# Later chunks of x, copies plus accumulating transfers in the first out-projection, a moved decay array, and w_down's copies at another place in the queue

## The chip, the core and the metric

The kernel runs on one core of one Trainium2 chip. Its engines work side by side, each on its own list of instructions in order: TensorE (PE, matrix products; PEld are its weight loads), VectorE (DVE), ScalarE (ACT), GpSimd (POOL) and SyncE (SP, which here only issues transfers). The metric is the device time of one execution in microseconds (us), as the median of several runs.

## The reference

One decoder layer on x with 2048 positions and 1024 channels, all in float32:

```python
h = rms_norm(x, norm1_g)
z = einsum('bsd,de->bse', h, w_in)              # 1024 -> 3584
lru_x, lru_gate, sc_b, sc_c, sc_x = split(z)    # 1024, 1024, 512, 512, 512
lru_x = causal_dwconv(lru_x, lru_conv_w) + lru_conv_b
y_lru = rg_lru(lru_x, ...) * gelu(lru_gate)     # gated linear recurrence over positions
y_sc = sc_b * causal_dwconv(sc_c * sc_x, sc_conv_w)
x = x + einsum('bse,ed->bsd', concat(y_lru, y_sc), w_out)    # 1536 -> 1024
h = rms_norm(x, norm2_g)
u = causal_dwconv(einsum('bsd,df->bsf', h, w_up), ffn_conv_w)    # 1024 -> 6144
gate, up = split(u)
x = x + einsum('bsf,fd->bsd', gelu(gate) * up, w_down)      # 3072 -> 1024
return rms_norm(x, final_g)
```

## The kernel before

Positions are worked in two halves of 1024 (T), and these in blocks of 512 (NB); channels lie on the 128 partitions. Every product is made exact enough by splitting both operands into a high part, a rounded copy by ScalarE (L233, names wh, fh, xh), and a low part, the difference by VectorE (L234, names wl, fl, xl), and adding three matmuls: high by high, high by low, low by high. So TensorE waits for a weight until a transfer (wr, wrw, wrf), ScalarE and VectorE have all done their part.

The stages, with the stretch of the profile: w_in for half 0 (0 to 337 us, `in_phase`, 28 products of 48 matmuls), the first out-projection (337 to 456), w_in for half 1 (456 to 752, `in_blocks`), the second out-projection (752 to 870), then w_up and w_down for half 0 and for half 1 (888 to 2250), and a tail. The stages after the first use a scheme with seven products of 2x2 blocks in place of eight; it needs sums of weight blocks and of operand blocks. The sums of w_out and w_down (so_d, sd_d) are made in HBM: `sum_step` has SyncE copy a block to its place and, two copies later, GpSimd add another block to it by an accumulating transfer (L409, L412). Each product of w_in's first stage calls `sum_step` once; for w_down, each pair j of the up stage calls it twice.

**In `in_phase`**, `beside_first(n)` stands beside the n-th product. It also makes the mean square of half 1 of x, in eight chunks xs0 to xs7 of 128 channels: load the chunk into one of two pages of 128 x 1024 (L1076, pages taken in turn by n % 2), square it (ScalarE, L1070 and L1072), add it up (VectorE, L1073, into ss_a). After the last it splits the sum, multiplies it by ones (four matmuls, ms_a) and takes the inverse root (`inv_rms`, a ScalarE table function ry_a and four VectorE operations). The loads stand in SyncE's queue between loads of w_in's weights (wr_in, L249).

**An out-projection (`sweeps`)** has seven sweeps of three steps. A step loads a weight block and an operand block (L1017), splits both, and does 24 matmuls into four PSUM banks (L1004). Odd sweeps go on adding into the same four banks (ox); even ones use banks of their own (oy). At a sweep's end its banks are added to or taken from the result pages xr (L1041, VectorE), which were loaded with x beforehand (`x_residual`, L586, SyncE):

```python
TAKEN = [[("11", 1, False)], [("12", 1, False), ("22", -1, False)],
         [("12", 1, False)], ...
```

"11", "12", "21" and "22" name the four quarters of the result, in two pages each (xr_11_0, xr_11_1); the first sweep is added to 11, the second to 12 and taken from 22. The loads of xr for 11 stand in the first sweep, those for 22 and 12 in the second, those for 21 in the last. Beside the steps, operands of a later stage are made (`x1_beside`, names hax, hbx, hcx; in the second out-projection `h_beside`, names ha, hb, at steps 4, 10, 15 and 19). `lru_scan` of the last channel group of half 1 runs at the opening of the second out-projection: its decay array a lies in one of two pages with tag "b", which xr_12's two pages use too.

The order of each engine's list is set by priorities (`high_priority(offset=...)`): an instruction with a larger offset is put as if it had been written so much earlier. Pages with a tag and a number of buffers (bufs) make a load wait until the last reader of the page's old contents is done, and SyncE's queue, being in order, holds all that stands behind such a load.

Of the kernel before, what the change touches and what calls it, by code (L numbers as in the profile page):

```python
# [14 lines left out]
S = 2048  # L15
# [16 lines left out]
GP = 0  # L32
UPP = 200
CP = 160
NS = 2
J0 = 2
LEAD = 5
# [56 lines left out]
def block_kernel(  # L94
# [282 lines left out]
    def lru_scan(c, half, cv, g, *gates, home=None, sign=1.0):  # L377
        n = f"{half}_{c}"
        r, i = (flat(p(f"{x}{n}")) for p, x in zip(home or (act, act), "ri"))
        a = big(f"a{n}", c % 2)[:, :T] if home else flat(act(f"a{n}"))  # L380
        with tc.high_priority(offset=HP):
            for k, (rows, ps) in enumerate(zip(HALVES, gates)):
                for b, p in enumerate(ps):
                    for dst, o, at in ((r, O_BA, k), (i, O_BX, 1 - k)):
                        nc.scalar.activation(
                            dst[rows, blk(b)], p[HALVES[at], :], AF.Sigmoid, bias=col(o + c)[rows, :]
                        )
        nc.vector.tensor_tensor(i, i, cv, ALU.mult)
        m = cv
        nc.scalar.activation(a, r, AF.Exp, scale=nc8[:, c : c + 1])  # L390
        nc.scalar.activation(m, r, AF.Tanh, scale=c8[:, c : c + 1])
        nc.scalar.activation(r, a, AF.Square)
        nc.vector.scalar_tensor_tensor(m, r, 1.0, m, ALU.add, ALU.mult)
        nc.scalar.activation(m, m, AF.Sqrt)
        nc.vector.tensor_tensor(i, i, m, ALU.mult)
        h = r
        init = 0.0 if half == 0 else h_last[:, c : c + 1]
        nc.vector.tensor_tensor_scan(h, a, i, init, ALU.mult, ALU.add)
        if half < NH - 1:
            nc.vector.tensor_copy(h_last[:, c : c + 1], h[:, T - 1 : T])  # L400
        nc.scalar.activation(g, g, AF.Gelu_apprx_tanh, scale=sign)
        y = g if home else h
        nc.vector.tensor_tensor(y, g, h, ALU.mult)
        return y
# [172 lines left out]
    def res_page(name, side):  # L577
        return ub.tile([P, 2, NB], F32, name=name, tag="ab"[side], bufs=2)

    def x_residual(half, alloc):  # L580
        def get(key, p):
            mh, t = PLACE[key]
            r = alloc(key, f"xr{half}_{key}_{p}")
            c = 4 * mh + 2 * p
            o = half * T + t * NB
            nc.sync.dma_start(r, xT[c : c + 2, :, o : o + NB].rearrange("m p c -> p m c"))  # L586
            return r

        return get

    def store_pair(dst, t, r, when=1):
        defer(when, dst[:, :, blk(t)].rearrange("m p c -> p m c"), r)
# [189 lines left out]
            a, c = even.pop()  # L782
            combine_odd(f_d[half], when, j // 2, a, cu, c, (cg[:, :NB], cg[:, NB:]))

    def up_phase(half, hs, between):
        with tc.high_priority(offset=UPP):
            wts = [up_weights(half, 0)]
        wts.append(up_weights(half, 1))
# [1 line left out]
        for j in range(NFF):  # L790
            if j + 2 < NFF:
                wts.append(up_weights(half, j + 2))
            nxt = UpPair(half, j + 1, hs, wts[j + 1]) if j + 1 < NFF else None
            if j == 0:
                cur.spread()
                nxt.begin()
                nxt.sum1()
            elif nxt is None:
                cur.middle(cur.sum1)
                cur.second()  # L800
                cur.fourth()
                cur.end()
            else:
                cur.middle(cur.second)
                nxt.begin()
                cur.fourth()
                if j + 2 < NFF:
                    nxt.sum1()
                cur.end()
            up_rest(half, j, cur.ug, cur.un)  # L810
            cur = nxt
            between(j)
# [169 lines left out]
                add = src[W_OPS.index(b), i2] if b in W_OPS else flat(dst[b][i2])  # L982
                pieces.append((t, src[W_OPS.index(a), i2], add))

    def sweeps(half, wsrc, fsrc, ni, name, residual, done, beside, tail=0, lead=0):
        res = {}
        fetch = {}
        for key, at in (("11", ((0, 1), (0, 2))), ("22", ((1, 0), (1, 0))), ("12", ((1, 2), (1, 2))), ("21", ((6, 1), (6, 1)))):
# [3 lines left out]
        for s, (wo, fo, on_x) in enumerate(SWEEPS):  # L992
# [42 lines left out]
            for m in range(4):  # L1035
                for h in held:
                    mm((m,), *h)
                for key, sign, final in TAKEN[s]:
                    r = res[key][m // 2][:, m % 2, :]
                    with tc.high_priority(offset=HE if not last else 2 * HP if m == 3 else HP):  # L1040
                        nc.vector.tensor_tensor(r, r, ps[m], ALU.add if sign > 0 else ALU.subtract)  # L1041
                    if final:
# [21 lines left out]
    def beside_first(n):  # L1064
        if n == 0:
            ss1[1] = acc_tile("a1")
        if 1 <= n <= KC:
            t = x1_raw.pop(n - 1)
            if n == 1:
                nc.scalar.activation(ss1[1], t, AF.Square)  # L1070
            else:
                nc.scalar.activation(t, t, AF.Square)  # L1072
                nc.vector.tensor_tensor(ss1[1], ss1[1], t, ALU.add)  # L1073
        if n < KC:
            t = x1_raw[n] = big(f"xs{n}", n % 2)[:, :T]
            nc.sync.dma_start(t, xT[n, :, T:S])  # L1076
        if n == KC:
            x1_raw["mean"] = mean_split(ss1[1], "a1")
        if n == KC + 2:
            inv_rms(ss1[1], "a1", x1_raw["mean"])  # L1080
        if n == -1:
            hx.append(x1_prep(0, ss1[1], 1))
# [31 lines left out]
    def res_alloc(key, n):  # L1114
# [9 lines left out]
        x_residual(0, res_alloc),  # L1124
        store_done(x2_d[0], None, "b0"),
        x1_beside,
    )

    rs2 = [[], []]
# [51 lines left out]

        return beside

    prepare = h_beside(0, (4, 10, 15, 19))

    def out1_beside(s):
        if s == 0:
# [12 lines left out]
        store_done(x2_d[1], None, "b1"),  # L1200
        out1_beside,
        lead=LEAD,
    )

    sums(w_down, sd_d, NI)
    mean1 = squares_then_mean(lambda k: x2_d[1][k // 2][k % 2], "b1", rs2[1], 2)

    def beside_pairs(j):
        mean1(j)
        for _ in range(NS if j >= J0 else 0):  # L1210
            sum_step()

    up_phase(0, hs[0], beside_pairs)

    ss3 = acc_tile("c0")

# [151 lines left out]
```

## Time and profile before

| what | value |
|---|---|
| median of 3 runs (lowest, highest) | 2262.89 us (2262.66, 2264.75) |
| profiled execution | 2264.07 us, its span 2262.3 us |
| mean granted clock of TensorE | 0.996 |
| TensorE, VectorE, ScalarE, GpSimd busy | 98%, 79%, 54%, 8% of the span |
| DMA queues: SyncE's, GpSimd's share of 16 engines | 45.7%, 9.5% |

In the profile a row of a timeline begins with its start and length in us, then engine, line, operation, output and inputs by the program's names with buffer numbers left out, and the number of instructions merged into it. In brackets stands how long the engine was idle just before, and what it waited for; "issue" means that the profile shows no reason. SPq is SyncE's queue. Adjacent rows of an engine may overlap by some 0.1 us, since the end of an instruction overlaps the next one's start.

### The profile page before, as it was taken

Reading aid. Unit: us, or ns where it says so; the run is one execution under the profiler, and the core shown is the slowest. Engines: PE = TensorE matmul, PEld = TensorE weight load, DVE = VectorE, ACT = ScalarE, POOL = GpSimd, SP = SyncE. Lnnn points to the kernel's source line nnn. Section 1 sums busy time; section 2 is a strip of 40 time slices with the busy share of each in tenths; the row PEclk is TensorE's granted clock in tenths of the full one; section 3 lists DMA queues with packets and bytes.
Section 4 is the critical chain, followed back from the end, with each engine's and each line's share of the span. In section 5 each row is a group of like instructions: output and inputs, shape, how many; then the busy total and the mean of one; then the engine's idle time right before and its main releaser. Section 6 shows DMA issues by size and latency. Waiting matters only on the chain.

```text
span 2262.3 us, 26386 instructions
## 1 busy us (share of the span) xinstructions
PE 2227.1 (98%) x9754; PEld 1818.2 (80%) x9754; DVE 1787.4 (79%) x2070; ACT 1214.6 (54%) x1404; POOL 174.1 (8%) x298
## 2 busy tenths in 40 slices
PE   9999999999999899999999999999999999999997
PEld 7787787888777688888888888888888888888886
DVE  8867879947777899898888887677988888876556
ACT  7638834547798554555454444444544444453343
POOL 0011110000100100111211100000000000000000
PEclk9999999999999999999999999999999999999999
DMA  7476357833533875588773267674233232359764
GB/s 281 149 228 188 110 212 267 305 100 125 186 117 109 310 258 184 163 251 236 209 179 112 98 216 269 228 252 147 88 104 118 91 111 93 112 194 345 246 196 153
DMA packets 157952, 415.00 MB, mean 183 GB/s; under 512 B 16640, under 2 KB 19328, under 8 KB 157248
## 3 DMA queue, kind: packets, MB, share of 16 engines
q1 hardware_dynamic: 136960, 356.96, 45.7%
q0 software_dynamic: 20720, 56.37, 9.5%
q8 instruction: 76, 1.25, 0.2%
q14 instruction: 52, 0.43, 0.1%
q10 hardware_dynamic: 144, 0.00, 0.0%
HBM read 311.55 MB, written 139.46 MB: 199 GB/s over the span
## 4 chain that ended last, share of the span: by engine, by line
PE 82%; DVE 6%; issue 6%; ACT 4%; DMA 2%; POOL 0%; SPq 0%; DVEq 0%; ACTq 0%; POOLq 0%
PE zx L671 21%; PE dx L1004 12%; PE zc L671 10%; PE zin_b L289 10%; PE dy L1004 9%; PE za L671 5%; PE ox L1004 5%; PE oy L1004 3%; PE zxin L671 2%; PE zS L671 1%; PE zcin L671 1%; PE zW L671 1%; DMA wrc_up<-in_w_up 1%; PE zain L671 1%; PE zr_b L374 1%
## 5 line engine op out<-in xcount | busy, mean ns | idle before, releaser
L234 DVE TENSOR_TENSOR fl_d<-wrf_d,fh_d 128x1024 fp32r<-128x1024 f32 x84 | 102.8, 1224 | 122.3 <-ACT fh_d L233 120.0
L233 ACT ACTIVATE fh_d<-wrf_d 128x1024 fp32r<-128x1024 f32 x84 | 89.0, 1059 | 202.1 <-PE dy L1004 78.5
L1004 PE MATMUL dx<-fh_d,wl_d 128*128 128x512 f32 x384 | 149.4, 389 | 0.0
L1004 PE MATMUL dx<-fl_d,wh_d 128*128 128x512 f32 x384 | 149.4, 389 | 0.0
L1004 PE MATMUL dx<-fh_d,wh_d 128*128 128x512 f32 x384 | 149.4, 389 | 0.0
L289 PE MATMUL zin_b<-xh,wl_in 128*128 128x512 f32 x448 | 138.8, 391 | 2.6 <-DVE wl_in L234 2.6
L289 PE MATMUL zin_b<-xh,wh_in 128*128 128x512 f32 x448 | 140.1, 394 | 0.0
L289 PE MATMUL zin_b<-xl,wh_in 128*128 128x512 f32 x448 | 138.9, 391 | 0.0
L234 DVE TENSOR_TENSOR wla_up<-wra_up,wha_up 128x1024 fp32r<-128x1024 f32 x48 | 58.8, 1225 | 100.9 <-ACT wha_up L233 100.9
L350 DVE SCALAR_TENSOR_TENSOR cg<-ug,prm,cg 128x1024 f32<-128x1024 f32 x96 | 123.1, 1282 | 9.4 <-ACT cg L346 8.5
L350 DVE SCALAR_TENSOR_TENSOR cu<-un,prm,cu 128x1024 f32<-128x1024 f32 x96 | 122.8, 1280 | 4.7 <-ACT cu L346 4.3
L671 PE MATMUL zc<-hhB,whd_up 128*128 128x512 f32 x368 | 120.8, 389 | 0.0
L671 PE MATMUL zx<-ht,whc_up 128*128 128x512 f32 x368 | 113.3, 389 | 0.0
L1004 PE MATMUL dy<-fh_d,wl_d 128*128 128x512 f32 x288 | 112.0, 389 | 0.0
L1004 PE MATMUL dy<-fl_d,wh_d 128*128 128x512 f32 x288 | 112.0, 389 | 0.0
L1004 PE MATMUL dy<-fh_d,wh_d 128*128 128x512 f32 x288 | 112.0, 389 | 0.0
L682 ACT ACTIVATE ug<-zx 128x512 f32<-128x512 f32 x92 | 54.8, 596 | 102.5 <-PE zx L671 102.1
L234 DVE TENSOR_TENSOR wl_d<-wrw_d,wh_d 128x1024 fp32r<-128x1024 f32 x84 | 102.5, 1220 | 8.4 <-ACT wh_d L233 7.0
L289 PEld LDWEIGHTS zin_b<-xh,wh_in 128*128 128x128 f32 x448 | 84.0, 189 | 23.4 <-DVE xl L425 1.5
L289 PEld LDWEIGHTS zin_b<-xh,wl_in 128*128 128x128 f32 x448 | 84.6, 189 | 20.7 <-DVE wl_in L234 3.1
L289 PEld LDWEIGHTS zin_b<-xl,wh_in 128*128 128x128 f32 x448 | 84.5, 189 | 18.0 <-DVE xl L458 0.4
L233 ACT ACTIVATE wha_up<-wra_up 128x1024 fp32r<-128x1024 f32 x48 | 50.9, 1060 | 82.8 <-PE zx L671 76.0
(549 smaller groups left out, 6384.4 us busy)
## 6 DMA issues: line engine op xcount, KB each, us to landing
wrc_up<-in_w_up SPq DMA_DIRECT2D x48, 512.0 KB, 4.9
f_d_T<-cg SPq DMA_DIRECT2D x96, 256.0 KB, 2.6
wrw_d<-sd_d_S SPq DMA_DIRECT2D x48, 512.0 KB, 4.5
wrf_d<-f_d_T SPq DMA_DIRECT2D x48, 512.0 KB, 4.2
f_d_B<-cu SPq DMA_DIRECT2D x72, 256.0 KB, 2.5
wrw_d<-in_w_down SPq DMA_DIRECT2D x36, 512.0 KB, 4.9
wrf_d<-f_d_B SPq DMA_DIRECT2D x36, 512.0 KB, 3.5
wr_in<-in_w_in SPq DMA_DIRECT2D x25, 512.0 KB, 7.1
```

The lines of the kernel that those rows point to most:

```text
L233: nc.scalar.activation(r32(hi), src, AF.Copy)
L234: nc.vector.tensor_tensor(r32(lo), src, hi, ALU.subtract)
L289: nc.tensor.matmul(ps[t], r32(a), r32(b[:, blk(t)]), start=(first and i == 0), stop=(last and i == 2))
L350: nc.vector.scalar_tensor_tensor(dst, src[:, k : k + T], col(o_w + k), dst, ALU.mult, ALU.add)
L374: nc.tensor.matmul(ps[t], gw[rows, :], cv[rows, blk(t)], start=True, stop=True)
L671: nc.tensor.matmul(ps, r32(p[:, s]), r32(self.hs[k][x][o]), start=f and i == 0, stop=l and i == 2, skip_group_check=True,)
L682: nc.scalar.activation(dst, self.x, AF.Copy)
L1004: nc.tensor.matmul(ps[m], r32(p), r32(x[:, k, :]), start=first and i == 0 and n == 0, stop=(last or not on_x) and i == ni - 1 and n == 2, ...
```

## The change

Four edits:

1. The loads of xs are no longer made beside products 0 to 7 but 0, 1, 3, 4, 5, 6, 7, 8; the mean's split comes beside product 9 and the inverse root beside product 11 (8 and 10 before).
2. In the first out-projection, the results 11, 12 and 22 get no load of x. At their first sweep, ScalarE copies the banks into the pages, with the sign as scale, and GpSimd then adds x to each page by an accumulating transfer from HBM. Six loads of SyncE and twelve adds of VectorE become six such transfers and twelve copies. Result 21, and the whole second out-projection, stay as they were.
3. The decay array of the last channel group's scan in half 1 is put into a page of another pool (`vpage`), away from xr_12's pages; the first `h_beside` of the second out-projection comes at step 5, not 4.
4. The two `sum_step`s of w_down stand ahead of the mean's loads (`mean1`) in an up pair, rather than behind them and the pair's other work beside it, and begin one pair later (j = 3, not 2).

```diff
+LATE = (("11", "12", "22"), ())
+LASTA = NLRU - 1
+XS_AT = (0, 1, 3, 4, 5, 6, 7, 8)
+XS_SIDE = 0
+XS_INV = 11
...
     def lru_scan(c, half, cv, g, *gates, home=None, sign=1.0):
-        a = big(f"a{n}", c % 2)[:, :T] if home else flat(act(f"a{n}"))
+        a = big(f"a{n}", c % 2)[:, :T] if home and c < LASTA else flat((act if not home else vpage)(f"a{n}"))
...
     def x_residual(half, alloc):
         def get(key, p):
             r = alloc(key, f"xr{half}_{key}_{p}")
-            nc.sync.dma_start(r, xT[c : c + 2, :, o : o + NB].rearrange("m p c -> p m c"))
+            if key not in LATE[half]:
+                nc.sync.dma_start(r, x_block(half, key, p))
             return r
+    def x_fills(half):
+        def fill(key, p, r):
+            nc.gpsimd.dma_start(r, x_block(half, key, p), accum_op=ALU.add)
+        return fill
...
-    def up_phase(half, hs, between):
+    def up_phase(half, hs, between, behind=lambda j: None):
...
             if j + 2 < NFF:
                 wts.append(up_weights(half, j + 2))
+            behind(j)
...
                 for key, sign, final in TAKEN[s]:
                     r = res[key][m // 2][:, m % 2, :]
+                    if fills and key in LATE[half] and not any(k == key for k, _, _ in sum(TAKEN[:s], [])):
+                        with tc.high_priority(offset=HE):
+                            nc.scalar.activation(r, ps[m], AF.Copy, scale=float(sign))
+                        if m % 2 == 1:
+                            fills(key, m // 2, res[key][m // 2])
+                        continue
...
     def beside_first(n):
-        if 1 <= n <= KC:
-            t = x1_raw.pop(n - 1)
-            if n == 1:
+        if n - 1 in XS_AT:
+            k = XS_AT.index(n - 1)
+            t = x1_raw.pop(k)
+            if k == 0:
...
-        if n < KC:
-            t = x1_raw[n] = big(f"xs{n}", n % 2)[:, :T]
-            nc.sync.dma_start(t, xT[n, :, T:S])
-        if n == KC:
+        if n in XS_AT:
+            k = XS_AT.index(n)
+            t = x1_raw[k] = big(f"xs{k}", (n + XS_SIDE) % 2)[:, :T]
+            nc.sync.dma_start(t, xT[k, :, T:S])
+        if n == XS_AT[-1] + 1:
             x1_raw["mean"] = mean_split(ss1[1], "a1")
-        if n == KC + 2:
+        if n == XS_INV:
             inv_rms(ss1[1], "a1", x1_raw["mean"])
...
-    prepare = h_beside(0, (4, 10, 15, 19))
+    prepare = h_beside(0, (5, 10, 15, 19))
...
-    def beside_pairs(j):
-        mean1(j)
-        for _ in range(NS if j >= J0 else 0):
+    def down_sums(j):
+        for _ in range(NS if j > J0 else 0):
             sum_step()
-    up_phase(0, hs[0], beside_pairs)
+    up_phase(0, hs[0], mean1, down_sums)
```

The change moves instructions on several engines; three places show how. First SyncE's queue in `in_phase`, around the third load of xs. Before (wr_in_21, wr_in_25 and so on are weights of w_in's products, so_d the copies for w_out's sums):

```order
L249 DMA wr_in_21_985<-in_w_in 128x1024
L409 DMA so_d_S_2_221<-in_w_out 16x8192
L1076 DMA xs_1045<-in_xT 128x1024
L249 DMA wr_in_25_1052<-in_w_in 128x1024
L409 DMA so_d_S_0_216<-in_w_out 16x8192
L249 DMA wr_in_17_1124<-in_w_in 128x1024
L409 DMA so_d_S_1_217<-in_w_out 16x8192
L249 DMA wr_in_2_1200<-in_w_in 128x1024
```

The same place in the changed kernel:

```order
L254 DMA wr_in_21_985<-in_w_in 128x1024
L414 DMA so_d_S_2_221<-in_w_out 16x8192
L254 DMA wr_in_25_1050<-in_w_in 128x1024
L414 DMA so_d_S_0_216<-in_w_out 16x8192
L254 DMA wr_in_17_1122<-in_w_in 128x1024
L414 DMA so_d_S_1_217<-in_w_out 16x8192
L254 DMA wr_in_2_1198<-in_w_in 128x1024
L414 DMA so_d_S_2_218<-in_w_out 16x8192
L1100 DMA xs_1268<-in_xT 128x1024
```

The third load of xs has gone from ahead of three weight loads to behind them.

Second, VectorE's list at the end of the first out-projection's second sweep. Before (oy_1 are that sweep's banks; wl_o and fl_o the low parts of the weight and operand of the step whose sweep and number follow; hlB, hlT and htx split operands of half 1's products):

```order
L234 TENSOR_TENSOR hlT1x_2867<-hcx_2852,hhT1x_2866 128x1024
L234 TENSOR_TENSOR htx_2870<-hqx_2853,htx_2870 128x512
L1041 TENSOR_TENSOR xr_12_0_2926<-xr_12_0_2926,oy_1_0_2802 128x512
L1041 TENSOR_TENSOR xr_22_0_2818<-xr_22_0_2818,oy_1_0_2802 128x512
L1041 TENSOR_TENSOR xr_12_0_2926<-xr_12_0_2926,oy_1_1_2803 128x512
L234 TENSOR_TENSOR wl_o_2_0_2967<-wrw_o_2_0_2962,wh_o_2_0_2966 128x1024
L1041 TENSOR_TENSOR xr_12_1_2928<-xr_12_1_2928,oy_1_2_2804 128x512
L234 TENSOR_TENSOR fl_o_2_0_2971<-wrf_o_2_0_2964,fh_o_2_0_2970 128x1024
L1041 TENSOR_TENSOR xr_22_1_2820<-xr_22_1_2820,oy_1_2_2804 128x512
L234 TENSOR_TENSOR wl_o_2_1_3003<-wrw_o_2_1_2998,wh_o_2_1_3002 128x1024
```

The same place in the changed kernel:

```order
L239 TENSOR_TENSOR wl_o_2_0_2967<-wrw_o_2_0_2962,wh_o_2_0_2966 128x1024
L239 TENSOR_TENSOR hlB11x_2857<-hax_2844,hhB11x_2856 128x1024
L239 TENSOR_TENSOR hlB21x_2861<-hbx_2845,hhB21x_2860 128x1024
L239 TENSOR_TENSOR hlT1x_2865<-hcx_2850,hhT1x_2864 128x1024
L239 TENSOR_TENSOR fl_o_2_0_2971<-wrf_o_2_0_2964,fh_o_2_0_2970 128x1024
L239 TENSOR_TENSOR wl_o_2_1_3003<-wrw_o_2_1_2998,wh_o_2_1_3002 128x1024
L239 TENSOR_TENSOR htx_2868<-hqx_2851,htx_2868 128x512
```

The adds into xr are gone from ahead of fl_o_2_0, and wl_o_2_0 now stands before the operands for half 1.

Third, GpSimd's list behind the last stores of y (y_d) of half 0. In the changed kernel:

```order
L235 DMA y_d_T_2_98<-yc_10_2509 128x512
L602 DMA xr_11_0_2734<-in_xT 128x2x512
L602 DMA xr_11_1_2771<-in_xT 128x2x512
L602 DMA xr_12_0_2924<-in_xT 128x2x512
L602 DMA xr_22_0_2818<-in_xT 128x2x512
L602 DMA xr_12_1_2925<-in_xT 128x2x512
L602 DMA xr_22_1_2819<-in_xT 128x2x512
L235 DMA x_d_0_263<-xr_12_0_2924 128x2x512
```

The six L602 rows are new here; before, the first x_d store followed the y_d store.

More of the change, by code (lines that the diff above doesn't have):

```diff
@@ L578, in res_page, with x_block @@
         return ub.tile([P, 2, NB], F32, name=name, tag="ab"[side], bufs=2)
+    def x_block(half, key, p):
+        mh, t = PLACE[key]
+        c = 4 * mh + 2 * p
+        o = half * T + t * NB
+        return xT[c : c + 2, :, o : o + NB].rearrange("m p c -> p m c")
     def x_residual(half, alloc):
         def get(key, p):
-            mh, t = PLACE[key]
             r = alloc(key, f"xr{half}_{key}_{p}")
-            c = 4 * mh + 2 * p
-            o = half * T + t * NB
-            nc.sync.dma_start(r, xT[c : c + 2, :, o : o + NB].rearrange("m p c -> p m c"))
-            return r
-        return get
+            if key not in LATE[half]:
+                nc.sync.dma_start(r, x_block(half, key, p))
+            return r
+        return get
+    def x_fills(half):
+        def fill(key, p, r):
+            nc.gpsimd.dma_start(r, x_block(half, key, p), accum_op=ALU.add)
+        return fill
     def store_pair(dst, t, r, when=1):
@@ L983, in sums, with sweeps @@
                 pieces.append((t, src[W_OPS.index(a), i2], add))
-    def sweeps(half, wsrc, fsrc, ni, name, residual, done, beside, tail=0, lead=0):
+    def sweeps(half, wsrc, fsrc, ni, name, residual, done, beside, tail=0, lead=0, fills=None):
         res = {}
@@ L1126, in block_kernel @@
         x1_beside,
+        fills=x_fills(0),
     )
@@ L1202, in block_kernel @@
         lead=LEAD,
+        fills=x_fills(1),
     )
```

## The prediction

> **What bounds the kernel now.** I read the busy shares on the page first, then the list of TensorE's waits, then the timelines around the longest of them.
>
> ```profile
> PE 2227.1 (98%) x9754; PEld 1818.2 (80%) x9754; DVE 1787.4 (79%) x2070; ACT 1214.6 (54%) x1404; POOL 174.1 (8%) x298
> PE oy L1004 <- DVE fl_o L234: 4.7, 3, 2.5
> PE ox L1004 <- DVE fl_o L234: 3.6, 2, 2.6
> PE zin_b L289 <- DVE wl_in L234: 2.6, 1, 2.6
> ```
>
> The first row gives busy time and share of each engine; the others give what TensorE waited for, in us altogether, times, and the longest. TensorE is busy for 2227.1 of 2262.3 us and no matmul is added or taken away, so the change can only win back waits and what they cause. The three rows hold 10.9 us: six waits, one while w_in's halves are multiplied, five in the two out-projections. Each is for VectorE to make the low part of an operand (wl_in or fl_o), so VectorE's order there decides, and whatever holds up VectorE.
>
> **Part 1: the chunks of x.** The queue's wait, and VectorE, ScalarE and TensorE around it:
>
> ```profile
> 46.70 0.69 DVE L277 TENSOR_TENSOR sb<-wr,sb 128x512 f32<-128x512 f32 x1
> SPq L1076 <- ACT ss_a L1070: 59.0, 1, 59.0
> 91.72 0.34 SPq L1076 DMA_DIRECT2D xs<-in_xT  x1
> 92.16 0.38 SPq L249 DMA_DIRECT2D wr_in<-in_w_in  x1
> 90.65 1.04 ACT L1070 ACTIVATE ss_a<-xs 128x1024 f32<-128x1024 f32 x1
> 102.13 1.06 ACT L233 ACTIVATE wh_in<-wr_in 128x1024 fp32r<-128x1024 f32 x1 [4.08 <-DMA wr_in<-in_w_in]
> 103.39 1.22 DVE L234 TENSOR_TENSOR wl_in<-wr_in,wh_in 128x1024 fp32r<-128x1024 f32 x1
> 104.66 0.73 PE L289 MATMUL zin_b<-xh,wl_in 128*128 128x512 f32 x2 [2.63 <-DVE wl_in L234]
> ```
>
> SyncE's queue issues nothing for 59.0 us: its third xs load needs the buffer of the first, which ScalarE's square frees only at 90.65 + 1.04 = 91.69. The weights queued behind it leave at 92.16 and land at about 102.1, which sets the split and TensorE's 2.63 us wait. In the new order this xs load stands behind three weight loads; the raw pages that the first two of these take are last read by the column sums around 46.70, so they go some 44 us earlier, and the third has two products, over 20 us, to spare. The wait goes, and the slower restart after it (0.1 us: 0.50 for the first matmul after a wait in the rows of part 2, where 0.39 is usual): 2.7.
>
> The wait has a second price:
>
> ```profile
> 103.00:110.00 7.00, 5.34 (x16) 4.26 (x17) 7.00 (x11) 3.37 (x4) 2.02 (x3) 0.76 1.03 383
> 160.00:252.00 92.00, 92.00 (x402) 71.81 (x402) 74.51 (x87) 78.25 (x82) 15.13 (x26) 1.00 0.55 160
> ```
>
> These are windows: length, busy time of each engine with its instructions, TensorE's granted clock, DMA share, GB/s. At full clock a matmul takes 92/402 = 0.229 us. After the wait 16 matmuls fill 110 - 104.66 = 5.34 us in place of 3.66: 1.7 us lost to a granted clock of 0.76 over the window. **Part 1 is worth 2.7 + 1.7 = 4.4 us.** The Trainium skill, page "TensorE: Matmul & The Clock Gate", section "Part 1: The HAM clock gate", says that the clock halves after at least one idle window of about 3.4 us, on a free-running grid. By it a wait of 2.63 us leaves the clock alone and this part gives only 2.7; the row shows the clock dropped, so the row decides.
>
> The shift also drags x's mean and inverse root (four DVE operations, 2 x 0.6 and 2 x 1.2 = 3.6 us, and a ScalarE table load) to the opening of the first out-projection, ahead of and around the third step's fl_o. Replayed with the durations of the rows, that fl_o ends about 0.2 us before TensorE asks for it. I take 0.3 us of wait, bounds 0 and 1.3 (one more operation ahead of it).
>
> **Part 2: the first out-projection's evictions.** In the profile:
>
> ```profile
> 351.34 2.05 DVE L1041 TENSOR_TENSOR xr<-xr,ox 128x512 f32<-128x512 f32 x3 [1.26 <-PE ox L1004]
> 358.63 1.22 DVE L234 TENSOR_TENSOR fl_o<-wrf_o,fh_o 128x1024 fp32r<-128x1024 f32 x1
> 359.91 0.50 PE L1004 MATMUL oy<-fl_o,wh_o 128*128 128x512 f32 x1 [0.90 <-DVE fl_o L234]
> 368.86 1.88 DVE L1041 TENSOR_TENSOR xr<-xr,oy 128x512 f32<-128x512 f32 x3 [1.51 <-PE oy L1004]
> 372.39 1.22 DVE L234 TENSOR_TENSOR fl_o<-wrf_o,fh_o 128x1024 fp32r<-128x1024 f32 x1
> 373.66 0.50 PE L1004 MATMUL ox<-fl_o,wh_o 128*128 128x512 f32 x1 [2.58 <-DVE fl_o L234]
> ```
>
> VectorE runs in order. Ahead of 351.34 and of 368.86 it stands idle 1.26 and 1.51 us until a product is finished, then adds it to x, and only then splits the operand that TensorE needs next. TensorE waits 0.90 and 2.58 us, and each restart costs a further 0.1: 3.7 together. In the new order the twelve adds are gone from VectorE, and with them 12 x 0.6 = 7.2 us. The second sweep's first fl_o (372.39 now) then waits only for ScalarE's half; replayed it ends near 367.7, while TensorE reaches it at 373.66 - 3.7 = 370.0. **Worth 3.7 us.** Below: 0, if ScalarE's copies make the fh_o late instead; against it stands
>
> ```profile
> L682 ACT ACTIVATE ug<-zx 128x512 f32<-128x512 f32 x92 | 54.8, 596 | 102.5 <-PE zx L671 102.1
> 350.00:400.00 50.00, 46.52 (x204) 37.90 (x203) 46.85 (x54) 22.93 (x24) 0.00 (x0) 1.00 0.69 233
> ```
>
> a copy of this shape at 596 ns, 12 x 0.6 = 7.2 us on an engine with 22.93 busy of 50, where VectorE has 46.85.
>
> What it adds: six transfers from GpSimd's queue that add x to the copies in place (512 KB each), for six plain loads that go. The trace has none into on-chip memory. The nearest are the accumulating transfers that add up weights in HBM, of the same size:
>
> ```profile
> 85.29 0.94 POOL L412 DMA_DIRECT2D so_d_S<-in_w_out  x1
> 92.00 0.90 POOL L412 DMA_DIRECT2D so_d_S<-in_w_out  x1 [5.77 <-issue]
> 103.94 0.88 POOL L412 DMA_DIRECT2D so_d_S<-in_w_out  x1 [11.04 <-issue]
> 956.12 0.95 POOL L412 DMA_DIRECT2D sd_d_S<-in_w_down  x1 [0.50 <-issue]
> 962.27 0.92 POOL L412 DMA_DIRECT2D sd_d_S<-in_w_down  x1 [5.20 <-DVE whd_up L234]
> so_d_S<-in_w_out POOLq DMA_DIRECT2D x5, 512.0 KB, 10.0
> sd_d_S<-in_w_down POOLq DMA_DIRECT2D x12, 512.0 KB, 6.1
> ```
>
> The last two rows are counts, size and median us to landing. One such transfer does not start before the last has landed: they start 6.7 and 11.9 us apart in the first stage, 6.15 in the second. So with L us from issue to landing, n of them take n x L + 0.3(n - 1). The three that matter are 12_0, 22_0 and 12_1, in this order, which can start when ScalarE has copied the second sweep's first products, about 369.5 on the clock of the rows above. VectorE adds the third sweep's products to page 12_1 in order, at about 387.3 (the sweep's 72 matmuls end near 386.1, and two adds of 0.6 stand before it). Behind those adds stands the fl_o for the second step of the fourth sweep: TensorE reaches it 24 matmuls, 5.4 us, after 386.1, at 391.5, and without a wait it ends at 386.1 + 4 x 0.6 + 1.2 = 389.7. There are 1.8 us to spare, so 12_1 must land by 389.1: 369.5 + 3L + 0.6 = 389.1, L = 6.3. Above that TensorE waits 3(L - 6.3).
>
> L depends on the load:
>
> ```profile
> 85.00:133.00 48.00, 45.37 (x194) 37.04 (x193) 42.56 (x52) 14.82 (x14) 8.20 (x12) 0.96 0.95 294
> 956.00:1062.00 106.00, 106.00 (x469) 87.78 (x468) 95.80 (x108) 56.77 (x68) 17.65 (x35) 1.00 0.83 231
> 368.00:391.00 23.00, 20.42 (x90) 16.61 (x89) 21.77 (x26) 8.28 (x9) 0.00 (x0) 1.00 0.70 240
> q0 software_dynamic: 3808, 7.34, 34.5%
> ```
>
> With 0.95 of the DMA engines busy the median is 10.0, with 0.83 it is 6.1. The last row is the accumulating queue's share over 950 to 1085, in which 14 were issued: 0.345 x 135/14 = 3.3 us of all 16 engines each. From 368 to 391 the share is 0.70 without them; three add 10 us to 16.1, which is all that 23 us can hold, though a part of the weight loads can slip. I take L = 7.3, between the two and nearer to the second, so 3 us of wait, bounds L = 5.6 (no wait) and 11.6 (16 us). The Trainium skill, page "DMA: Bandwidth & Descriptors", section "Anatomy of one DMA — SWDGE (gpsimd) path", fits 2.0 us plus the bytes over 436 GB/s to such a queue's transfers: an estimate of 3.2 us here and no wait. No transfer of this size and kind in this trace landed near that.
>
> **Part 3: the second out-projection.**
>
> ```profile
> 767.45 5.11 SPq L586 DMA_DIRECT2D xr<-in_xT  x2
> 772.61 0.46 SPq L1017 DMA_DIRECT2D wrw_o<-so_d_S  x1
> 776.76 0.50 PE L1004 MATMUL oy<-fl_o,wh_o 128*128 128x512 f32 x1 [2.51 <-DVE fl_o L234]
> 782.55 1.23 DVE L234 TENSOR_TENSOR fl_o<-wrf_o,fh_o 128x1024 fp32r<-128x1024 f32 x1
> 783.83 0.50 PE L1004 MATMUL oy<-fl_o,wh_o 128*128 128x512 f32 x1 [1.29 <-DVE fl_o L234]
> 790.55 0.50 PE L1004 MATMUL ox<-fl_o,wh_o 128*128 128x512 f32 x1 [0.99 <-DVE fl_o L234]
> ```
>
> The second x load of the pair stood until the scan let go of the page that its decay array held; with the array elsewhere the weights behind it leave about 4 us earlier. In the new order the fl_o of 782.55 stands ahead of the four adds of xr_11 (2.4 us at 0.6 each), and h's first chunk comes a step later: the 783.83 wait goes, 1.4 with its restart. The 776.76 wait hangs on the scan, which still runs before it; the 790.55 one on stores of y. Both stay. **Worth 1.4**, bounds -1.3 (the chunk moves its delay on to the next step) and 2.7.
>
> **Part 4: w_down's copies**, moved by a pair and ahead of the sx loads, stand between the same stores and the same w_up loads. TensorE's wait there is
>
> ```profile
> 1113.08 0.50 PE L671 MATMUL zx<-hhB,whc_up 128*128 128x512 f32 x1 [1.50 <-ACT ug L682]
> ```
>
> I take 0: the copies go out behind a pair's matmuls, and without that cover cost about another such wait. Bounds -1.6 and +1.6.
>
> **Sum.** -4.4 + 0.3 - 3.7 + 3 - 1.4 = -6.2 on the profiled run's 2264.07 (span 2262.3 and 1.8 around it): 2257.9. That run lies 1.2 above the median 2262.89, so I predict **2256.7**. One halved-clock window more or less is 1.7.
>
> **Rivals.** *No wait for the fills* (L up to 6.3, as between 956 and 1062): 2256.7 - 3 - 0.3 = 2253.4. For it: six plain loads leave the stretch or the one before it. Against: the 10 us of DMA time.
> *Fills at the crowded rate*, L 8.5 to 9.5: waits of 6.6 to 9.6, with a halved window 8.3 to 11.3 against the 3 above: 2262 to 2265, no change. For it: the 10.0 row.
> *Slower: fills one by one in a full queue.* The mechanism is the same in-order add of 12_1 ahead of fl_o; without any fill wait the sum is 2253.7, so it loses once the wait and its clock pass 9.2 us, L near 8.8, and is clearly slower (2267.4) from L near 10.3. At the 11.6 of the rows 92.00 to 103.94: 16 + 1.7 more, 2271.4. Against it: that stretch held 0.95 before one fill came, this one 0.70.
> *The change doesn't cure the out-projection*: VectorE, at 46.85 of 50, is late by its operand chain, not by the adds, or the copies hold up fh_o: the 3.7 stays and the sum is 2260.4, no change. Against it: its idle 1.26 and 1.51 just before the adds.
>
> **Chances.** Forecast 0.42, no wait 0.22, crowded 0.15, slower 0.11, not cured 0.10. A measurement tells 0.2%, 4.5 us: faster is below 2258.4. The forecast's own range, 2254 to 2260, lies below it for most of its chance (0.35 of 0.42), all of the second does, and 0.03 of the others: 0.60. Slower 0.12, the rest 0.28. The range 2250.5 to 2264.5 holds the forecast, the second and the two that end level, and leaves out the slower one and the tails.
>
> **What would show it.** Right: no wait for wl_in near 104 and a clock of 1.00 in that window; SyncE issuing weights between 48 and 90; no fl_o wait in the first two sweeps' steps near 359 and 373; GpSimd rows of xr<-in_xT six to eight us apart; a wait for fl_o near 390 of about 3 us. Wrong: GpSimd's fills far apart (slow) or issued back to back (no chain at all); a new wait in the opening steps at 345 to 350; clock drops elsewhere, as at the 776.76 wait, which now costs none.

## The result: slower by 0.4%, and the profile after

| | before | changed |
|---|---|---|
| median of 4 runs each, us | 2263.82 (2262.66 to 2265.41) | 2274.24 (2272.87 to 2275.10) |
| profiled execution and its span, us | 2264.07, 2262.3 | 2273.72, 2271.9 |
| ratio of the runs, 95% interval | | 1.0037 (1.0022 to 1.0051) |

The changed kernel is slower by 8.4 us by the ratio (5.0 to 11.5; the medians of the table differ by 10.4). 2256.7 was forecast, in a range of 2250.5 to 2264.5, and the time lies above it. Measured from the first matmul of each stage to that of the next in the two traces, the difference of the spans, 9.6 us, goes where this table puts it:

| stage | before | changed | difference |
|---|---|---|---|
| w_in, half 0 | 331.1 | 326.3 | -4.8 |
| first out-projection | 118.3 | 129.2 | +10.9 |
| w_in, half 1 | 296.9 | 296.3 | -0.6 |
| second out-projection | 120.0 | 120.3 | +0.3 |
| w_up, half 0 | 459.8 | 464.2 | +4.4 |
| everything after | 930.4 | 929.9 | -0.5 |

The page and the list of TensorE's waits of the changed kernel:

```profile
PE 2229.6 (98%) x9754; PEld 1819.2 (80%) x9754; DVE 1778.9 (78%) x2058; ACT 1219.0 (54%) x1415; POOL 183.6 (8%) x304
PE oy L1020 <- DVE fl_o L239: 13.9, 3, 11.1
PE zx L686 <- ACT ug L697: 3.9, 2, 2.5
PE ox L1020 <- DVE fl_o L239: 1.4, 3, 0.8
```

The wait for wl_in is gone from the list, the waits for ox fell from 3.6 to 1.4 us, and one wait for oy of 11.1 us is new. Three views show what that one is: GpSimd's timeline, then VectorE's and TensorE's, then four windows.

```profile
348.33 1.25 POOL L602 DMA_DIRECT2D xr<-in_xT  x1 [22.98 <-ACT xr L1058]
358.91 1.23 POOL L602 DMA_DIRECT2D xr<-in_xT  x1 [9.33 <-ACT hhT1x L238]
370.51 1.19 POOL L602 DMA_DIRECT2D xr<-in_xT  x1 [10.38 <-PE ox L1020]
380.78 1.20 POOL L602 DMA_DIRECT2D xr<-in_xT  x1 [9.08 <-ACT wh_o L238]
390.62 1.19 POOL L602 DMA_DIRECT2D xr<-in_xT  x1 [8.64 <-ACT wh_o L238]
396.99 1.20 POOL L602 DMA_DIRECT2D xr<-in_xT  x1 [5.17 <-issue]
383.07 1.27 DVE L1063 TENSOR_TENSOR xr<-xr,ox 128x512 f32<-128x512 f32 x2
396.76 1.28 DVE L1063 TENSOR_TENSOR xr<-xr,ox 128x512 f32<-128x512 f32 x2 [12.42 <-DMA xr<-in_xT]
397.96 1.22 DVE L239 TENSOR_TENSOR fl_o<-wrf_o,fh_o 128x1024 fp32r<-128x1024 f32 x1
387.72 0.39 PE L1020 MATMUL oy<-fh_o,wh_o 128*128 128x512 f32 x1
399.24 0.79 PE L1020 MATMUL oy<-fl_o,wh_o 128*128 128x512 f32 x1 [11.13 <-DVE fl_o L239]
```

The six rows of xr<-in_xT are the accumulating transfers 11_0, 11_1, 12_0, 22_0, 12_1 and 22_1. Each is issued some 0.3 us after the one before it has landed: 10.6, 11.6, 10.3, 9.8 and 6.4 us apart. VectorE has added to page 12_0 at 383.07 and then stands for 12.42 us at the add to 12_1, whose transfer was issued only at 390.62 and landed at 396.67. The fl_o behind that add ends at 399.2, and TensorE, which had nothing left to do from 388.1 (387.72 + 0.39), goes on in the same instant. The columns of the windows are length, busy time of PE, PEld, DVE, ACT and POOL with instructions, granted clock, DMA share, GB/s:

```profile
340.00:360.00 20.00, 20.00 (x90) 16.51 (x89) 19.73 (x20) 11.74 (x14) 2.34 (x2) 1.00 0.75 229
370.00:381.00 11.00, 10.36 (x45) 7.93 (x44) 10.21 (x11) 9.30 (x11) 1.41 (x2) 1.00 1.02 337
391.00:397.00 6.00, 0.00 (x0) 0.00 (x0) 0.24 (x1) 0.00 (x0) 0.83 (x2) 0.50 0.67 122
398.00:404.00 6.00, 4.76 (x11) 3.80 (x12) 6.00 (x7) 0.00 (x0) 0.19 (x1) 0.50 0.80 180
```

Up to 360 TensorE never stops. While the DMA engines are full (1.02) a transfer takes 9.5 to 11.3 us from issue to landing; when SyncE's queue has nearly run dry (0.67, of which its own transfers are 0.08) the fifth takes 6.05. The granted clock also halves during the wait, and TensorE pays for that until 404: 11 matmuls in the last row, 4.76 us after it restarted, where full speed gives 21.

### The profile page after: what moved, and what is told of

Read it like the earlier page. It is cut to its first block, busy times and chain, and to the rows that moved or that the text cites. A ratio compares the mean times of both kernels' runs of the same rounds, so it can differ in the third digit from the quotient of the medians.

```text
span 2271.9 us, 26392 instructions
## 1 busy us (share of the span) xinstructions
PE 2229.6 (98%) x9754; PEld 1819.2 (80%) x9754; DVE 1778.9 (78%) x2058; ACT 1219.0 (54%) x1415; POOL 183.6 (8%) x304
## 3 DMA queue, kind: packets, MB, share of 16 engines
q0 software_dynamic: 22352, 59.52, 10.3%
## 4 chain that ended last, share of the span: by engine, by line
PE 77%; issue 7%; DVE 6%; ACT 6%; DMA 3%; POOL 1%; SPq 1%; DVEq 0%; POOLq 0%; ACTq 0%
PE zx L686 20%; PE dx L1020 11%; PE zc L686 10%; PE dy L1020 9%; PE zin_b L294 8%; PE za L686 5%; PE ox L1020 3%; PE oy L1020 3%; PE zxin L686 3%; DMA wrc_up<-in_w_up 1%; PE zcin L686 1%; PE zS L686 1%; ACT r L390 1%; PE zW L686 1%; PE zain L686 1%
## 5 line engine op out<-in xcount | busy, mean ns | idle before, releaser
L238 ACT ACTIVATE fh_d<-wrf_d 128x1024 fp32r<-128x1024 f32 x84 | 89.0, 1059 | 205.5 <-PE dy L1020 78.5
L355 DVE SCALAR_TENSOR_TENSOR cg<-ug,prm,cg 128x1024 f32<-128x1024 f32 x96 | 122.8, 1279 | 10.6 <-ACT cg L351 9.8
```

The source lines that it names most:

```text
L238: nc.scalar.activation(r32(hi), src, AF.Copy)
L355: nc.vector.scalar_tensor_tensor(dst, src[:, k : k + T], col(o_w + k), dst, ALU.mult, ALU.add)
```

## The experiments

Each kernel was timed in turns with the kernel before on the same chip; ratios are to that kernel, with 95% intervals, and 0.1% is 2.3 us. A diff is against the changed kernel, unless it is said to be added to the kernel before; `...` stands for lines left out.

### One edit at a time

The first edit alone, as what has to be taken back from the changed kernel:

```diff
-LATE = (("11", "12", "22"), ())
+LATE = ((), ())
-LASTA = NLRU - 1
+LASTA = NLRU
-    prepare = h_beside(0, (5, 10, 15, 19))
+    prepare = h_beside(0, (4, 10, 15, 19))
...
-    up_phase(0, hs[0], mean1, down_sums)
+    up_phase(0, hs[0], beside_pairs)
```

> The kernel before with the first edit alone (chunks of x at products 0, 1, 3 to 8, mean and inverse root a product later). Theory, from the two profiles: the first stage shortens from 331.1 to 326.3 us and nothing else moves, so 4 to 5 us faster than before, about 0.998. Rival: the mean and inverse root that now run at the opening of the first out-projection push its operand splits back, and part or all of the gain is lost there: 0 to 3 us faster.

Measured: 0.9979 (0.9971 to 0.9988), 4.8 us faster. Its first stage takes 326.3 us, as in the changed kernel, and at the opening of the first out-projection, where the mean's work now stands, TensorE does not stop (first row). The wait of 0.90 us at the second sweep's first fl_o, which part 2 of the prediction counts, is gone with this edit too. What is left is the wait of the second sweep's end, which here costs a clock window too, seen as 71 matmuls in 17.42 us of busy time:

```profile
331.90:360.00 28.10, 27.97 (x124) 22.85 (x123) 27.06 (x31) 11.90 (x14) 0.00 (x0) 1.00 0.94 349
360.00:380.00 20.00, 17.42 (x71) 13.90 (x70) 19.65 (x23) 8.40 (x9) 0.00 (x0) 0.91 0.74 251
368.25 0.50 PE L1020 MATMUL ox<-fl_o,wh_o 128*128 128x512 f32 x1 [2.58 <-DVE fl_o L239]
```

The second edit alone:

```diff
-XS_AT = (0, 1, 3, 4, 5, 6, 7, 8)
+XS_AT = (0, 1, 2, 3, 4, 5, 6, 7)
-XS_INV = 11
+XS_INV = 10
...
```

with the third and fourth taken back as above.

> The kernel before with the second edit alone (copies by ScalarE, six accumulating transfers). Theory: the transfers run one after the other at about 10 us each while the queue of weights fills the DMA engines, the third sweep's add waits for the fifth of them, and the first out-projection grows from 118.3 to about 129 us: 10 to 12 us slower. Rival: the long transfers come from the work that the first edit moved into the same stretch; without it they land in 6 to 7 us, and the stage is level with before or up to 4 us shorter.

Measured: 1.0042 (1.0030 to 1.0054), 9.5 us slower, a little less than the theory had; the stage takes 126.1 us, not 129. The rival falls: without the first edit's work the transfers are as far apart, 8.1 to 11.1 us between each two of the first five, and the wait is there.

```profile
373.73 1.19 POOL L602 DMA_DIRECT2D xr<-in_xT  x1 [6.83 <-ACT wh_o L238]
383.54 1.20 POOL L602 DMA_DIRECT2D xr<-in_xT  x1 [8.62 <-ACT fh_o L238]
394.55 1.19 POOL L602 DMA_DIRECT2D xr<-in_xT  x1 [9.80 <-ACT fh_o L238]
PE oy L1020 <- DVE fl_o L239: 13.9, 3, 10.1
```

The third edit alone, added to the kernel before:

```diff
-        a = big(f"a{n}", c % 2)[:, :T] if home else flat(act(f"a{n}"))
+        a = big(f"a{n}", c % 2)[:, :T] if home and c < LASTA else flat((act if not home else vpage)(f"a{n}"))
-    prepare = h_beside(0, (4, 10, 15, 19))
+    prepare = h_beside(0, (5, 10, 15, 19))
```

> The kernel before with the third edit alone (decay array in another page, h's first chunk at step 5). Theory: the waits of 1.5 and 1.2 us in the second out-projection go (2.6 us), and the stage's change beyond that, +0.4 in all in the changed kernel, was a halved clock window (1.7 us) and some smaller waits: 0 to 3 us faster. Rival: the edit does nothing for the time but shifts the waits: within 1 us of before, in every profile.

Measured: 0.9996 (0.9988 to 1.0005): 0.9 us faster, between 2.7 faster and 1.1 slower. The second out-projection took 120.4 us, 120.0 before, though the wait of 783.83 is gone: the wait of 776.76, which stays, now goes with a halved clock. That of 790.55 stays as well, 0.80 us where it was 0.99.

```profile
777.30 0.69 PE L1020 MATMUL oy<-fl_o,wh_o 128*128 128x512 f32 x1 [2.48 <-DVE fl_o L239]
777.40:780.90 3.50, 3.50 (x9) 2.72 (x10) 3.50 (x6) 1.06 (x1) 2.26 (x5) 0.51 0.94 321
790.85 0.50 PE L1020 MATMUL ox<-fl_o,wh_o 128*128 128x512 f32 x1 [0.80 <-DVE fl_o L239]
```

In the profile before, a wait of 2.51 us at the same place left the clock alone. The wait of 2.58 us at the end of the second sweep in the first out-projection, which this edit does not touch, also halved the clock here and not in the profile before; so a halved window more or less need not come from the edit. The edit takes away the wait that it was aimed at, and the run doesn't tell its worth from nothing: it lies within both the theory and the rival.

The fourth edit alone, added to the kernel before (`down_sums` as in the change):

```diff
...
-    up_phase(0, hs[0], beside_pairs)
+    up_phase(0, hs[0], mean1, down_sums)
```

> The kernel before with the fourth edit alone (w_down's copies ahead of the mean's loads and a pair later). Theory: the waits for w_up's operands near 1113 and 1200 us (1.7 and 0 before, 2.7 and 1.5 in the changed kernel) come from this edit: 2.5 us slower, 4.4 if a clock window is halved too. Rival: they come from where the stage happens to start after the other edits: level with before, within 1 us.

Measured: 1.0009 (1.0001 to 1.0018), 2.0 us slower (0.2 to 4.1). The first up stage took 462.3 us, not 459.8. Rows of the kernel before, then of this one:

```profile
1100.00:1110.00 10.00, 10.00 (x46) 8.29 (x45) 5.79 (x7) 4.70 (x5) 0.56 (x1) 1.00 0.88 284
```

```profile
1100.00:1110.00 10.00, 10.00 (x45) 8.26 (x44) 7.47 (x9) 5.15 (x6) 1.85 (x3) 1.00 0.97 258
1115.91 0.80 PE L686 MATMUL zx<-hhB,whc_up 128*128 128x512 f32 x1 [2.57 <-ACT ug L697]
1110.00:1120.00 10.00, 7.43 (x27) 5.75 (x26) 8.05 (x9) 4.16 (x5) 1.96 (x3) 0.83 0.47 110
```

The wait of 1.50 us has become 2.57, and with it comes a halved window (0.83). In these windows the DMA engines look fuller, 0.97 to 0.88, but the wait stands 2.8 us later in this profile; taken at the same distance, 16 to 6 us ahead of the wait, the shares are 0.96 and 0.95. So it is not shown that fuller engines make the wait longer. The four ratios alone add up to 5.8 us slower, the change as a whole to 8.4 (5.0 to 11.5), which their intervals allow.

### The transfers taken back, made plain, put in another order

The changed kernel without the second edit:

```diff
-LATE = (("11", "12", "22"), ())
+LATE = ((), ())
```

> The changed kernel with the second edit taken back (plain loads of x, all adds on VectorE), the other three kept. Theory: the first out-projection goes back to about 118.3 us from 129.2, so 2274.2 - 10.9 = 2263, level with before: the gain of the first edit (4.8) and the loss in the first up stage (4.4) cancel. Rival: the other edits together also lose in the first out-projection, and this stays 3 us or more slower than before.

Measured: 0.9994 (0.9983 to 1.0004), level with before as the theory has it, and about 10 us below the changed kernel. The first out-projection took 119.2 us. The profiled execution is the slowest of this kernel's, 2270.43 us against a median of 2263.97, and its first up stage takes 469.3 us, 9.5 more than in the kernel before. Three waits there are longest: 1.83 us near 1059, 3.29 near 1116, and one of 2.00 with a halved window at a place where the kernel before had none:

```profile
1195.17 0.50 PE L686 MATMUL zx<-hhB,whc_up 128*128 128x512 f32 x1 [2.00 <-ACT ug L697]
1190.00:1200.00 10.00, 8.00 (x28) 6.10 (x28) 10.00 (x12) 3.38 (x5) 1.91 (x3) 0.83 0.00 1
```

Transfers without accumulation:

```diff
-            nc.gpsimd.dma_start(r, x_block(half, key, p), accum_op=ALU.add)
+            nc.gpsimd.dma_start(r, x_block(half, key, p))
```

> The changed kernel with GpSimd's six transfers made plain: they overwrite the pages with x rather than adding to them, so the first products are left out of the results 11, 12 and 22. Theory: what makes a chain of them is the accumulation; plain ones of the same bytes from the same queue are issued as soon as their pages are ready, land in 4 to 8 us side by side, and the wait of 11.3 us goes: about 13 us faster than the changed kernel, 2261. Rival: GpSimd's queue itself takes one at a time, or the full DMA engines alone make them 10 us long: the wait stays within 3 us of 11.3.

Measured: 0.9976 (0.9967 to 0.9985), 5.4 us faster than before. The first out-projection takes 114.28 us: 504 matmuls at 0.227 and no wait.

```profile
349.01 0.73 POOL L602 DMA_DIRECT2D xr<-in_xT  x1 [21.71 <-ACT xr L1058]
351.13 0.73 POOL L602 DMA_DIRECT2D xr<-in_xT  x1 [1.39 <-ACT xr L1058]
365.63 1.43 POOL L602 DMA_DIRECT2D xr<-in_xT  x2 [13.78 <-PE oy L1020]
368.19 0.71 POOL L602 DMA_DIRECT2D xr<-in_xT  x1 [1.13 <-ACT xr L1058]
373.56 0.72 POOL L602 DMA_DIRECT2D xr<-in_xT  x1 [4.67 <-DMA xr<-in_xT]
xr<-in_xT POOLq DMA_DIRECT2D x6, 512.0 KB, 8.4
```

This is the run that parts the two halves of the trouble. Plain transfers of the same bytes from the same queue are long too, a median of 8.4 us, with the DMA engines about as full (0.84 to 1.02 from 348 to 381). But the first two go out 2.1 us apart, and three go out within 2.6 us at 365 to 368, so they run side by side, and the third of that group, 12_1, has landed at 379.3, in time. Only the sixth waits for a landing, that of the third at 373.26. It is the accumulation that makes them go one at a time; the program does not order them, since in the changed kernel's trace none of them waits for the semaphore of the one before it.

Accumulation also costs the DMA engines more: GpSimd's queue holds 31.1% of them from 348 to 397 in the changed kernel, 16.5% here. That lighter load alone would not have saved the stage. At 8.4 us each and one after another, 12_1 would have landed near 392, an estimate from these rows, and VectorE needs it by about 385 (389.1 in the prediction, less 4.1 for the earlier start of the stage).

Another order of the same six:

```diff
-            held = []
+            held, late = [], []
...
                         if m % 2 == 1:
-                            fills(key, m // 2, res[key][m // 2])
+                            late.append((key, m // 2, res[key][m // 2]))
+                        if m == 3 and key == TAKEN[s][-1][0]:
+                            for f in sorted(late):
+                                fills(*f)
                         continue
```

> The changed kernel with the order of the transfers changed: both pages of 12 before those of 22, so that the one waited for is the fourth of the chain and not the fifth. Theory: it lands one transfer, 6 to 10 us, earlier, the wait of 11.3 us falls to 2 to 5, and the kernel is 6 to 10 us faster than the changed one, 2264 to 2268. Rival: the wait does not hang on the transfers' order but on the load of the DMA engines, and stays.

Measured: 1.0021 (1.0012 to 1.0030), 4.8 us slower than before, so some 4 us better than the changed kernel and short of the 6 to 10 expected:

```profile
370.70 1.19 POOL L602 DMA_DIRECT2D xr<-in_xT  x1 [10.29 <-DVE hcx L631]
381.69 1.20 POOL L602 DMA_DIRECT2D xr<-in_xT  x1 [9.79 <-issue]
392.79 1.19 POOL L602 DMA_DIRECT2D xr<-in_xT  x1 [9.90 <-issue]
395.03 0.79 PE L1020 MATMUL oy<-fl_o,wh_o 128*128 128x512 f32 x1 [7.48 <-DVE fl_o L239]
```

Page 12_1 is now the fourth transfer, issued at 381.69, but this one takes the full load's 10.8 us, where the fifth took 6.05 on an emptier machine. TensorE's wait falls from 11.13 to 7.48.

### The wait without the add, and a better kernel

The changed kernel without the third sweep's adds to result 12:

```diff
+                    if fills and LATE[half] and s == 2:
+                        continue
                     with tc.high_priority(offset=HE if not last else 2 * HP if m == 3 else HP):
                         nc.vector.tensor_tensor(r, r, ps[m], ALU.add if sign > 0 else ALU.subtract)
```

> The changed kernel without VectorE's four adds of the third sweep's products to result 12 in the first out-projection (these products are left out of the result); the six accumulating transfers stay. Theory: TensorE waits only because fl_o stands in VectorE's list behind an add that needs the fifth transfer; without these adds the transfers are as long as before (9 to 11 us) but nobody waits for them, the wait of 11.3 us goes, and the first out-projection takes 115 to 117 us in place of 129: 12 to 14 us faster than the changed kernel, 2260 to 2262. Rival: the full DMA engines make the weights late as well, and waits of 4 us or more remain in that stage.

Measured: 0.9989 (0.9979 to 0.9998), 2.5 us faster than before and 10.9 better than the changed kernel, a little less than expected; the stage takes 116.8 us, within the 115 to 117 of the theory. Windows of the first out-projection, of the changed kernel and of this one:

```profile
332.00:447.00 115.00, 103.23 (x442) 84.20 (x442) 94.24 (x100) 59.35 (x68) 7.67 (x7) 0.94 0.84 269
```

```profile
332.00:447.00 115.00, 113.39 (x498) 92.85 (x497) 100.00 (x109) 63.95 (x76) 8.76 (x8) 1.00 0.90 291
380.83 1.20 POOL L602 DMA_DIRECT2D xr<-in_xT  x1 [9.36 <-ACT wh_o L238]
391.89 1.19 POOL L602 DMA_DIRECT2D xr<-in_xT  x1 [9.86 <-issue]
```

The transfers are as far apart as before (11.1 us here), and TensorE loses 1.6 us rather than 11.8. So the transfers hurt through the one place in VectorE's list that needs 12_1, with fl_o behind it, and hardly through late weights. The run also spares VectorE four adds of about 0.6 us, too little for a gain of 10.9.

That suggested filling only what is needed later. The changed kernel with

```diff
-LATE = (("11", "12", "22"), ())
+LATE = (("11", "22"), ())
```

> The changed kernel with 12 loaded and added to as before, and only 11 and 22 filled late. Theory: no transfer of the chain is needed before the fourth sweep ends, the wait of 11.3 us goes, and with four adds left on VectorE in the second sweep of the first out-projection most of the two old waits (4.0 us) stay away: 2274.2 - 13 to 15 = 2259 to 2261. Rival: the four transfers still fill the DMA engines at 350 to 390 and make the weights late: 2263 or more.

Measured: 0.9971 (0.9961 to 0.9981), 6.6 us faster than before. The first out-projection takes 115.0 us:

```profile
332.00:447.00 115.00, 114.55 (x506) 94.47 (x504) 105.97 (x120) 62.59 (x73) 6.36 (x6) 1.00 0.88 293
```

Then the same with the fourth edit taken back too:

```diff
...
-    up_phase(0, hs[0], mean1, down_sums)
+    up_phase(0, hs[0], beside_pairs)
```

> The kernel with only 11 and 22 filled late, and w_down's copies back at their old place (first and third edit kept). Theory: the fourth edit costs 2 to 4.5 us in the first up stage, which goes back from 463 to about 460.5 us: 2255 to 2257.5, ratio to the kernel before 0.9955 to 0.9965. Rival: the long first up stages hung on the moment at which that stage starts, not on the edit; the time stays within 1 us of the 0.9971 of the kernel with the fourth edit.

Measured: 0.9965 (0.9952 to 0.9977). And without the third and the fourth, so with this on top:

```diff
-LASTA = NLRU - 1
+LASTA = NLRU
...
-    prepare = h_beside(0, (5, 10, 15, 19))
+    prepare = h_beside(0, (4, 10, 15, 19))
```

> The same without the third edit: first edit, 11 and 22 filled late, nothing else. Theory: the third edit takes two waits (2.6 us) from the second out-projection but leaves one of 2.7 that halves the clock in some runs, so it is worth 1 to 2.5 us: this one is slower by that, 0.9965 to 0.9975. Rival: the third edit is worth nothing, and this one is as fast.

Measured: 0.9963 (0.9949 to 0.9977). The intervals of these three overlap almost wholly. The kernel without the fourth edit lies at the edge of its expected 0.9955 to 0.9965, the one also without the third just outside its 0.9965 to 0.9975; so neither theory is borne out, and neither is ruled out. Their profiles show one thing that blurs the comparison: the wait in the first up stage is there with the fourth edit or without it, and its length varies. Of the kernel without the fourth edit, then of the one without the third and fourth:

```profile
PE zx L686 <- ACT ug L697: 2.9, 1, 2.9
```

```profile
PE zx L686 <- ACT ug L697: 1.3, 1, 1.3
```

All three beat both kernels by a margin that holds.

## Why the prediction was wrong, point by point

**Part 1, -4.4 us: right.** The stage is 4.8 us shorter and the edit alone 4.8 us faster. Both prices were there, the wait and the halved clock: the changed kernel's queue now sends the next weights from 45 us on, and the clock stays at 1.00 where it was 0.76.

```profile
45.37 0.33 SPq L254 DMA_DIRECT2D wr_in<-in_w_in  x1
100.00:110.00 10.00, 10.00 (x45) 8.26 (x44) 10.00 (x15) 2.13 (x2) 1.47 (x2) 1.00 0.86 231
```

The rule of the Trainium skill (page "TensorE: Matmul & The Clock Gate", section "Part 1: The HAM clock gate") gave 2.7 for this part, since no full idle window passed; the stage's 4.8 decides against it here. The 0.3 us allowed for the moved mean were not needed: no wait shows at the opening of the out-projection.

**Part 2, the two waits, -3.7 us: right in size, the cause in part.** Neither wait is there in the changed kernel, and the stage takes 114.3 to 117.6 us in the five runs above in which nothing waits for the transfers, against 118.3. But the wait of 0.90 us also goes with the first edit alone, so 1.0 of the 3.7 needs no change to the adds. And the sum left the clock out here: the wait of 2.58 us halved it in three of the five profiles that still have this wait, though not in the profile before (why, see the end). That the gain comes near 3.7 is partly luck.

**Part 2, the transfers, +3 us: the term that failed.** The mechanism was named, with its place: transfers one by one, the add to 12_1 in VectorE's order, fl_o behind it. Two steps of the working failed.

The first is L, the time from issue to landing. 7.3 us was chosen between 6.1 and 10.0, on the argument that 0.70 of the DMA engines' time was in use in that stretch; the transfers took 10.2, 11.3, 9.9, 9.5 and 6.05 us. The same working had 10 us for three transfers beside 16.1 already in use: 26 us, where the stretch holds 23, and not "all that 23 us can hold". That is a full machine, and the row measured on one was 10.0.

The second is the start of the chain. It was put at the moment when 12_0's copies are ready, as if the two transfers for result 11 were out of the way by then. With L = 7.3 they would have been: landed at 363.2, and the copies ready at about 364.5. At 10.2 and 11.3 they held 12_0 back to 370.51, 6.0 us.

Then came 370.51 to 396.67 for three, 8.5 each with the gaps taken off: by the prediction's formula 3 x (8.5 - 6.3) = 6.6. Together that is 12.6, against a wait of 11.13; TensorE came to that place about 1.4 us later than the working had it (388.1, against 391.5 less the 4.8 of part 1). So nearly half of the wait comes from the late start, for which the prediction had no term. The wait's whole price in the stage was 11.1 us of idle time and 2.5 for the clock, half of the 4.9 us after the restart; two short waits for fl_o ahead of it, 0.21 and 0.44 us, are new too.

The rival "fills one by one in a full queue", given a chance of 0.11 and 2271.4 us, comes nearest, and its mechanism is the one that the runs show. Its sum is not: its three transfers alone, at 8.5, stay below the 8.8 from which it loses, and the late start makes up the rest.

The estimate by the Trainium skill's page "DMA: Bandwidth & Descriptors", section "Anatomy of one DMA — SWDGE (gpsimd) path", of 3.2 us and no wait is far from any of the six transfers: the shortest took 6.05 us.

**Part 3, -1.4 us: the waits went as said, the gain did not show.** The 783.83 wait went; those of 776.76 and 790.55 stayed, as expected, the second at 0.78 us. The stage is no shorter: the wait of 2.5 us that stayed halved the clock in five of the six profiles that have it with the edit, and in none of the four without. The clock had been named as a possible loss at that place, with no term of its own. Whether the edit brings that about or only the moment at which the wait falls (see the end) is not shown. Alone the edit measured 0.9 us faster, with an interval that holds both 1.4 and nothing.

**Part 4, 0 us: mis-sized.** Alone it cost 2.0 us (0.2 to 4.1); in the changed kernel's profile the stage is 4.4 us longer:

```profile
1119.96 0.50 PE L686 MATMUL zx<-hhB,whc_up 128*128 128x512 f32 x1 [2.53 <-ACT ug L697]
1200.50 0.50 PE L686 MATMUL zx<-hhB,whc_up 128*128 128x512 f32 x1 [1.33 <-ACT ug L697]
```

1.50 us have become 2.53 with a halved window, and a second wait stands near 1200. The bound of 1.6 was one more wait of the size seen, and left out the clock that goes with it. The stage took 462.3 to 469.3 us in the seven profiles with the edit (465.1 on average) and 458.8 to 462.7 in the six without (460.9), one execution each, so the profiles point to some 4 us; the timed runs show 2.0 for the edit alone, and no clear difference between the two kernels above with it and without. How the edit makes the waits stays open: the one near 1110 differed widely with the edit (1.2 to 3.3 us) and without it (from under 0.7 to 3.2); the one near 1186 to 1200 was seen only with it, in four of the seven.

**The chances.** The forecast's centre added the terms of parts 1 and 2, which came out, to one that was far down the range of what its own rows showed. The break-even of 8.8 us that the rival gave lay below the 10.0 of the nearest row; that row should have carried the forecast. Even the rival priced only three transfers of a chain of five.

## What to carry to other kernels

In these runs a transfer that adds into its destination was no cheap replacement for a load: several of them form a chain, so what counts is the sum of their times from the first of the chain to the one that is needed first, at the DMA load that they make themselves. Give that way only to results that are needed late, and keep an in-order engine's urgent work ahead of whatever reads them. When a stage has two or three TensorE waits, removing some can change whether the rest halve the clock, so size a bound with the clock in it.

## What the runs showed of the hardware that was not expected

- Accumulating transfers from GpSimd's queue into on-chip memory are issued one at a time, 0.3 us after the last has landed, as those between HBM buffers were in the profile before; plain ones from the same queue run side by side (2.1 us apart with 8 us to landing).
- In the changed kernel's profile such a transfer of 512 KB took 9.5 to 11.3 us with the DMA engines at 0.89 to 1.02, 6.05 and 6.4 us with less under way.
- The same wait of 2.58 us for fl_o at the end of the second sweep left the clock at 1.00 in the profile before (at 373.66) and halved it for 3.4 us in the kernel with the first edit alone (at 368.25); a wait of 11.13 us had the clock at half for 4.9 us after it ended.
- The clock records of the traces say what parts the two. Within a trace the halved stretches begin on a grid of 3.413 us (in the profile before at 105.94 and 631.59, 154 steps apart). In the 13 profiles, between 40 and 2235 us, the clock fell from full 31 times, each time after a grid step in which TensorE had been idle for 1.90 us or more; the longest idle times in a step that no drop followed were 1.93 and 1.88. Of the 2.58 us before 373.66, 1.48 lay in one step; of those before 368.25, 2.29. So in these traces a wait of 2.5 us halves the clock or not by where it falls on the grid: it leaves the clock alone where both its parts are under 1.9 us, in some 1.3 of the 3.4 us, so it halves the clock in about 6 placements of 10, by this estimate.
